# Weight chunks of four 128x512 blocks, one raw tile per seven-product unit, and a residual kept in DRAM during the FFNs

## The chip, the cores and the metric

The kernel runs on one core of a Trainium2 chip. The metric is the device time of one execution in microseconds (us), as the median of several runs. TensorE is written PE, its loads of the stationary operand PEld, VectorE DVE, ScalarE ACT, GpSimd POOL and SyncE SP. SP issues nearly all DMAs.

## The reference, cut to what matters

One layer: a half-step gated FFN, a mixer of two gated linear attentions, a second half-step FFN, each with a norm before and after and a residual. 256 rows, width 2048, FFN width 5504, float32.

```python
def swiglu(x, w_gate, w_up, w_down):
    return (jax.nn.silu(x @ w_gate) * (x @ w_up)) @ w_down

f1 = swiglu(rms_norm(h, ffn1_pre_norm), ffn1_w_gate, ffn1_w_up, ffn1_w_down)
h = h + 0.5 * rms_norm(f1, ffn1_post_norm)
m = hybrid_token_mixer(rms_norm(h, mix_pre_norm), ...)   # proj = u @ w_in; two scans; two branches; w_out
h = h + rms_norm(m, mix_post_norm)
f2 = swiglu(rms_norm(h, ffn2_pre_norm), ffn2_w_gate, ffn2_w_up, ffn2_w_down)
h = h + 0.5 * rms_norm(f2, ffn2_post_norm)
```

## The kernel before, in words

**Split products.** A float32 product is made of three matmuls of a rounded format: each operand is split into `hi`, its rounded value, and `lo = x - hi`; the sum is hi*hi + lo*hi + hi*lo (`mm3`, L155 to L159). Weights come from DRAM into `raw` tiles. ACT writes `whi` as a rounding copy (L151) and DVE subtracts to get `wlo` (L153). All weights are read once, so all of them go through this splitting.

**Tiles.** Rows are two tiles of 128 (`t`), the contraction goes in k-tiles of 128 (`kt`), columns in blocks of 512 (`CB`). A `raw`, a `whi` and a `wlo` tile hold two blocks of 128x512 each (`RW = 2 * CB`), and there are five of each (`RING = 5`). A chunk is two blocks. SP issues a chunk's load as soon as a raw tile is free, so SP runs ahead by the number of raw tiles; ACT and DVE split a chunk as soon as its raw data have landed and a hi/lo pair is free, so they run ahead of PE by the number of hi/lo pairs.

**Two column blocks at a time.** `gemm_pair` makes two column blocks together (gate and up, or two blocks of `w_in`). The contraction is in units `u` of two k-tiles. A plain unit is 2 matrices x 2 k-tiles x 2 row tiles x 3 matmuls, that is 24 matmuls, done in two halves of one matrix each. A unit in `sevens` is a 2x2x2 block product by seven products in place of eight (`Blocks.seven`, L265): 21 matmuls, but three sums of weight blocks (`wsum`) are added on DVE and split as well. `SUMS` has three such units of eight, `FOUR` four. In an FFN they alternate from one pair to the next, the first pair has none; in the mixer, eight of the ten pairs use `SUMS` and two `FOUR`. `gemm_pair` writes the order of the plain halves and of the sevens out by hand (`steps`, `at`); with `late` the sevens come at the end. After the last unit, `share` and `close` add the shared products to the results on DVE. `following` splits the first chunks of the next pair before the closing sums.

**FFN.** Eleven pairs make the gated activations in `hT` (11 tiles, through silu on ACT, one product on DVE into `hn`, and transposes on PE). `down_proj` takes 43 k-tiles by two halves of 1024 columns, `hf`, with six seven-product units in each. The last seven k-tiles of the second half (`DTAIL`) are split ahead and kept, in ring tiles and in tiles that hold nothing else by then (`homes`), because their matmuls come in four passes, one for each row tile and column block.

**Mixer.** `gemm_block` with `held` makes a block for row tile 0 while row tile 1's input is still being settled. Ten pairs of `w_in` blocks follow with the attention between them as side work (`side.pump`), then four `w_branch_gla` and four `w_branch_hgrn` blocks, and `out_proj`. The residual `h` (8 tiles of 128x512) stays on chip in the FFNs; at the mixer's start it is stored to `away` in DRAM, and `h` serves as scratch.

**Order.** Instructions are issued in each engine's queue in an order that a list scheduler fixes at compile time, by the order in which the program states them and by when their inputs would be ready. At run time each queue is in order. DMAs on SP wait in its queue for their raw tile.

Of the kernel before, what the change touches and what calls it, by code (L numbers as in the profile page):

```python
# [7 lines left out]
F32 = mybir.dt.float32  # L8
# [7 lines left out]
P = 128  # L16
# [11 lines left out]
RW = 2 * CB  # L28
STEPS = ((3, 2, 2, 2), (6, 1, 1, 1))
RING = 5  # L30
AHEAD = 3
# [55 lines left out]
def kernel(ctx: ExitStack, tc: tile.TileContext, a: dict, out: bass.AP):  # L87
# [22 lines left out]
    h = [[hpool.tile([P, CB], F32, name=f"h{t}_{n}") for n in range(4)] for t in range(NT)]  # L110

    away = [[dram.tile([P, CB], F32, name=f"away{t}_{n}") for n in range(4)] for t in range(NT)]
# [10 lines left out]

    def ring_alloc(w):
        hi, lo = [ring.tile([P, RW], F32R, tag=s, name=nm(s))[:, :2 * w]
                  .rearrange("p (i c) -> p i c", i=2) for s in ("whi", "wlo")]
        return [(hi, lo)]

    def wload(src: bass.AP, w: int, apart=False):
        raw = ring.tile([P, RW], F32, tag="raw", name=nm("raw"))[:, :2 * w].rearrange(  # L130
            "p (i c) -> p i c", i=2)
        for i in range(2) if apart else [slice(0, 2)]:
            nc.sync.dma_start(raw[:, i, :], src[:, i, :])
        return raw, apart

    def wchunk(src: bass.AP, w: int, alloc=ring_alloc, raw=None):


        raw, apart = raw or wload(src, w)
        parts = alloc(w)  # L140
        if len(parts) == 1:
            hi, lo = parts[0]
            for i in range(2) if apart else [slice(0, 2)]:
                split_into(hi[:, i, :], lo[:, i, :], raw[:, i, :])
            return [(hi[:, i, :], lo[:, i, :]) for i in range(2)]
        for i, (hi, lo) in enumerate(parts):
            split_into(hi, lo, raw[:, i, :])
        return parts
# [12 lines left out]
    def gemm_block(w_dram, c0, w, lhs, nkt=KT, held=None, raws=(), ready=()):  # L161
# [4 lines left out]
        raws, ready = list(raws), list(ready)  # L166
        nb = -(-w // CB)
        step = 2 // nb
        pss = [[ps_tile(f"mm{t}") for _ in range(nb)] for t in range(NT)]

        def chunk(k0, alloc):
            if ready:
                return ready.pop(0)
            raw = raws.pop(0) if raws else None
            src = w_dram[k0 * P:(k0 + step) * P, c0:c0 + w]
            return wchunk(src.rearrange("(k p) c -> p k c", p=P) if nb == 1 else
                          src.rearrange("p (n c) -> p n c", n=nb), w // nb, alloc, raw)

        def mm(t, k0, parts):
            for i, part in enumerate(parts):  # L180
                kt = k0 + i % step
                mm3(pss[t][i // step][:, :w // nb], lhs(t, kt), part, kt == 0, kt == nkt - 1)

        if held is None:
            for k0 in range(0, nkt, step):
                parts = chunk(k0, ring_alloc)
                for t in range(NT):
                    mm(t, k0, parts)
                side.pump()
        else:  # L190
            kept = []
            for i, k0 in enumerate(range(0, nkt, 2)):
                kept.append((k0, chunk(k0, ring_alloc if i < RING else held)))
                mm(0, *kept[-1])
                side.pump()
            for k in kept:
                mm(1, *k)
                side.pump()
# [46 lines left out]
    class Blocks:  # L245
# [19 lines left out]
        def seven(self, u, end):  # L265
            w, k0 = self.w, 2 * u
            ra, rb = [ring.tile([P, RW], F32, tag="raw", name=nm("raw"))[:, :2 * w]
                      .rearrange("p (i c) -> p i c", i=2) for _ in range(2)]
            wsum, hi, lo = [row_tile(n, d)[:, :, :w] for n, d in
                            (("wsum", F32), ("wsumh", F32R), ("wsuml", F32R))]  # L270

            nc.sync.dma_start(ra[:, 0, :], self.block(0, k0))
            nc.sync.dma_start(ra[:, 1, :], self.block(1, k0 + 1))
            nc.sync.dma_start(rb[:, 0, :], self.block(1, k0))
            nc.sync.dma_start(rb[:, 1, :], self.block(0, k0 + 1))
# [8 lines left out]
            last[0] = nc.scalar.activation(hi[:, 2, :], wsum[:, 2, :], AF.Copy)  # L284
# [4 lines left out]
            first, second, third = [[(part[0][:, i, :], part[1][:, i, :]) for i in range(n)]  # L289
                                    for part, n in (((ahi, alo), 2), ((bhi, blo), 2), ((hi, lo), 3))]  # L290
# [5 lines left out]
            self.product((0, 0), self.lhs(0, k0 + 1), second[1])  # L296
            side.pump()
            self.product("p6", self.part("s2", u), second[0], end)
            self.product("p5", self.part("d", u), third[0], end)
            self.product("p7", self.part("s3", u), third[1], end)  # L300
# [1062 lines left out]
```

## Time and profile before

| | |
|---|---|
| median of 3 runs | 2080.19 us (2079.95 to 2080.34) |
| profiled execution | 2080.67 us |
| span of its instructions | 2078.8 us |
| PE busy | 2067.8 us (99%), 10509 matmuls |
| DVE busy | 1854.7 us (89%), 2187 instructions |
| ACT busy | 1239.7 us (60%), 1670 instructions |
| DMA | 412.23 MB, 198 GB/s in the mean |

A row of groups gives line, engine, operation, the tiles as out<-in, the shape and the number of instructions; then busy time and mean ns of one; then the idle time of the engine just before them and what ended most of it. A row of waits gives who waited <- for whom: us in total, times, longest. A row of the timeline gives start and duration. A row of stretches gives busy time (and count) of each engine, the granted clock of PE, the DMA share and GB/s. Durations of matmuls overlap; their price is the distance of their starts.

### The profile page before, as it was taken

To read this page: it belongs to the slowest core of one execution; us is meant where nothing else is said; L and a number is where in the kernel's file an instruction comes from. 1 tells how busy PE (TensorE), PEld (TensorE's weight loads), DVE (VectorE), ACT (ScalarE), POOL (GpSimd) and SP (SyncE) were. 2 spreads that over 40 slices of the span, in tenths; PEclk is the share of its full clock that TensorE was granted. 3 is DMA by queue.
4 is the path that set the end of the run, shared out by engine and by line. 5 is a ranking of instruction groups with operands and counts; after the bars stand their busy time and mean duration, and the time that the engine had idled before them with its cause. 6 is when DMAs were issued, how large, how long until landed. Compare 5 with 4: busy or idle time off the path is not lost.

```text
span 2078.8 us, 29319 instructions
## 1 busy us (share of the span) xinstructions
PE 2067.8 (99%) x10509; PEld 1721.1 (83%) x10509; DVE 1854.7 (89%) x2187; ACT 1239.7 (60%) x1670; POOL 40.6 (2%) x87
## 2 busy tenths in 40 slices
PE   9999999999999999999999999999999999999998
PEld 7888888898888888878888888888888888898886
DVE  7898999989999879989999897578999989999896
ACT  6555656565666576576655554465555655666663
POOL 1000000000000100000000000010000000000000
PEclk9999999999999999999999999999999999999999
DMA  8566656656667467555565666755666657576663
GB/s 267 183 210 199 211 188 194 214 183 226 208 195 233 153 192 232 163 168 188 174 203 186 184 221 214 220 179 172 222 200 186 209 186 224 165 239 201 198 208 132
DMA packets 200665, 412.23 MB, mean 198 GB/s; under 512 B 18036, under 2 KB 26423, under 8 KB 200520
## 3 DMA queue, kind: packets, MB, share of 16 engines
q1 hardware_dynamic: 194896, 401.80, 61.0%
q10 hardware_dynamic: 5624, 8.57, 1.3%
q8 instruction: 82, 1.34, 0.3%
q14 instruction: 63, 0.52, 0.1%
HBM read 406.11 MB, written 4.19 MB: 197 GB/s over the span
## 4 chain that ended last, share of the span: by engine, by line
PE 96%; ACT 1%; DVE 1%; issue 0%; DMA 0%; POOL 0%; SPq 0%; DVEq 0%; POOLq 0%; ACTq 0%
PE c L157 22%; PE c L159 21%; PE c L158 21%; PE p L159 5%; PE p L158 5%; PE p L157 5%; PE mm L157 3%; PE mm L159 3%; PE mm L158 3%; PE ps L397 2%; PE acc L157 1%; PE acc L158 1%; PE acc L159 1%; PE ps L905 0%; DVE h L510 0%
## 5 line engine op out<-in xcount | busy, mean ns | idle before, releaser
L151 ACT ACTIVATE whi<-raw 128x1024 fp32r<-128x1024 f32 (+3 forms) x498 | 510.6, 1033 | 279.8 <-PE c L158 114.7
L153 DVE TENSOR_TENSOR wlo<-raw,whi 128x1024 fp32r<-128x1024 f32 (+3 forms) x498 | 587.5, 1190 | 86.6 <-ACT whi L151 85.3
L157 PE MATMUL c<-whi,xhi 128*128 128x512 f32 (+1 forms) x1270 | 495.8, 391 | 0.5 <-DVE hq L849 0.3
L159 PE MATMUL c<-wlo,xhi 128*128 128x512 f32 (+1 forms) x1270 | 490.8, 387 | 0.0
L158 PE MATMUL c<-whi,xlo 128*128 128x512 f32 (+1 forms) x1270 | 490.5, 386 | 0.0
L243 DVE TENSOR_TENSOR wlo<-raw,whi 128x1024 fp32r<-128x1024 f32 (+1 forms) x252 | 294.5, 1203 | 11.9 <-ACT whi L278 6.3
L159 PEld LDWEIGHTS c<-wlo,xhi 128*128 128x128 f32 x1270 | 238.4, 188 | 47.2 <-DVE wlo L153 0.3
L157 PEld LDWEIGHTS c<-whi,xhi 128*128 128x128 f32 x1270 | 238.5, 188 | 46.9 <-issue 0.7
L158 PEld LDWEIGHTS c<-whi,xlo 128*128 128x128 f32 x1270 | 238.6, 188 | 44.9
L282 ACT ACTIVATE whi<-raw 128x1024 fp32r<-128x1024 f32 (+1 forms) x126 | 131.8, 1046 | 204.5 <-DVE raw L243 78.5
L243 DVE TENSOR_TENSOR wsuml<-wsum,wsumh 128x1536 fp32r<-128x1536 f32 (+1 forms) x126 | 218.0, 1730 | 33.7 <-ACT wsumh L284 33.6
L157 PE MATMUL c<-whi,hkhi 128*128 128x512 f32 x558 | 217.0, 389 | 0.0
L159 PE MATMUL c<-wlo,hkhi 128*128 128x512 f32 x558 | 216.8, 388 | 0.0
L158 PE MATMUL c<-whi,hklo 128*128 128x512 f32 x558 | 216.7, 388 | 0.0
L280 ACT ACTIVATE wsumh<-wsum 128x1024 fp32r<-128x1024 f32 (+1 forms) x126 | 131.5, 1044 | 108.6 <-DVE wsum L243 74.7
L278 ACT ACTIVATE whi<-raw 128x1024 fp32r<-128x1024 f32 (+1 forms) x126 | 131.4, 1043 | 100.2 <-PE c L158 84.7
L243 DVE TENSOR_TENSOR wsum<-raw,raw 128x1024 f32<-128x1024 f32 (+1 forms) x126 | 151.8, 1205 | 20.5 <-DMA raw<-in_ffn_w_down_dram 17.3
L159 PEld LDWEIGHTS c<-wlo,hkhi 128*128 128x128 f32 x558 | 104.8, 188 | 21.6
L158 PEld LDWEIGHTS c<-whi,hklo 128*128 128x128 f32 x558 | 104.8, 188 | 21.3
L157 PEld LDWEIGHTS c<-whi,hkhi 128*128 128x128 f32 x558 | 104.8, 188 | 21.3
L243 DVE TENSOR_TENSOR c<-c,psum 128x512 f32<-128x512 f32 (+1 forms) x135 | 86.6, 682 | 11.8 <-PE c L159 11.4
L243 DVE TENSOR_TENSOR wsum<-raw 128x512 f32<-128x512 f32 (+1 forms) x126 | 86.0, 683 | 3.6
(347 smaller groups left out, 3117.1 us busy)
## 6 DMA issues: line engine op xcount, KB each, us to landing
raw<-in_ffn_w_down_dram SPq DMA_DIRECT2D x124, 512.0 KB, 4.6
raw<-in_w_in_dram SPq DMA_DIRECT2D x104, 512.0 KB, 4.5
raw<-in_ffn_w_up_dram SPq DMA_DIRECT2D x97, 512.0 KB, 4.5
raw<-in_ffn_w_gate_dram SPq DMA_DIRECT2D x96, 512.0 KB, 4.7
raw<-in_ffn_w_gate_dram SPq DMA_DIRECT2D x128, 256.0 KB, 3.8
raw<-in_w_in_dram SPq DMA_DIRECT2D x128, 256.0 KB, 3.5
raw<-in_ffn_w_up_dram SPq DMA_DIRECT2D x126, 256.0 KB, 3.8
raw<-in_ffn_w_down_dram SPq DMA_DIRECT2D x96, 256.0 KB, 4.0
```

Of the source, the lines that this page charges most:

```text
L151: last[0] = nc.scalar.activation(hi, src, AF.Copy)
L153: nc.vector.tensor_tensor(lo, src, hi.bitcast(F32), op=ALU.subtract)
L157: nc.tensor.matmul(ps, lhsT=xhi, rhs=whi, start=start, stop=False)
L158: nc.tensor.matmul(ps, lhsT=xlo, rhs=whi, start=False, stop=False)
L159: nc.tensor.matmul(ps, lhsT=xhi, rhs=wlo, start=False, stop=stop)
L243: return nc.vector.tensor_tensor(o, x, y, op=op)
L278: nc.scalar.activation(ahi, ra, AF.Copy)
L280: nc.scalar.activation(hi[:, 0:2, :], wsum[:, 0:2, :], AF.Copy)
L282: nc.scalar.activation(bhi, rb, AF.Copy)
L397: end = nc.tensor.transpose(dst_ps[:, i * P:(i + 1) * P], src[:, i * P:(i + 1) * P], ident)
```

## The change

`RW` becomes `4 * CB`: raw, hi and lo tiles hold four blocks. There are three hi/lo pairs (`RING = 3`) and two raw tiles (`RAWS = 2`). The residual becomes two tiles `hrow` of 128x2048, of which `h[t][n]` are slices, under the tag `hold`; while `roomy` is set, in an FFN from its second pair on, these two serve as raw tiles three and four in turn. The second FFN stores the residual to `away2` first; `residual()` loads it back (in the first FFN from `x`) after unit 6 of the second half of `down_proj`, and from there on `roomy` is off. A plain unit is one chunk of both matrices, loaded by two DMAs and split by one ACT and one DVE instruction; in `seven`, all four blocks are in one raw tile, rearranged so that three are split to `hi` by one instruction, and `lo` by one. `gemm_block`, `out_proj` and `down_proj` take chunks of four blocks as well. The FFN's `hn` is gone, its product overwrites silu's tile; `hT` has 10 tiles, its last part lies in `xlo0`; the mixer has 31 tiles `b` for 33.

```diff
-RW = 2 * CB
+RW = 4 * CB
-RING = 5
-AHEAD = 3
+RING = 3
+RAWS = 2
+AHEAD = 2
...
+    def new_h():
+        for t in range(NT):
+            hrow[t] = hpool.tile([P, 4, CB], F32, tag="hold", name=nm(f"h{t}"), bufs=NT)
+            h[t] = [hrow[t][:, n, :] for n in range(4)]
...
+    def raw_tile(w):
+        turn[0] += 1
+        if roomy[0] and turn[0] % (RAWS + NT) >= RAWS:
+            raw = hpool.tile([P, RW], F32, tag="hold", name=nm("raw"), bufs=NT)
+        else:
+            raw = ring.tile([P, RW], F32, tag="raw", name=nm("raw"), bufs=RAWS)
+        return raw[:, :4 * w].rearrange("p (i c) -> p i c", i=4)
...
+    def split(raw, w, n=4, alloc=ring_alloc):
+        parts, at = [], 0
+        for hi, lo in alloc(w):
+            m = min(hi.shape[1], n - at)
+            split_into(hi[:, :m, :], lo[:, :m, :], raw[:, at:at + m, :])
+            parts += [(hi[:, i, :], lo[:, i, :]) for i in range(m)]
+            at += m
         return parts
...
         def seven(self, u, end):
-            ra, rb = [ring.tile([P, RW], F32, tag="raw", name=nm("raw"))[:, :2 * w]
-                      .rearrange("p (i c) -> p i c", i=2) for _ in range(2)]
...
-            (ahi, alo), (bhi, blo) = ring_alloc(w) + ring_alloc(w)
-            nc.scalar.activation(ahi, ra, AF.Copy)
-            add(wsum[:, 0:2, :], ra, rb[:, 0:1, :].broadcast_to([P, 2, w]))
-            nc.scalar.activation(hi[:, 0:2, :], wsum[:, 0:2, :], AF.Copy)
-            add(rb[:, 0, :], wsum[:, 0, :], ra[:, 1, :])
-            nc.scalar.activation(bhi, rb, AF.Copy)
-            summed = add(wsum[:, 2, :], rb[:, 0, :], rb[:, 1, :])
-            last[0] = nc.scalar.activation(hi[:, 2, :], wsum[:, 2, :], AF.Copy)
+            raw = raw_tile(w)
...
+            for j, (i, k) in enumerate(((0, k0), (1, k0 + 1), (0, k0 + 1), (1, k0))):
+                load(raw, j, self.block(i, k))
+
+            hi, lo = ring_alloc(w)[0]
+            nc.scalar.activation(hi[:, 0:3, :], raw[:, 0:3, :], AF.Copy)
+            add(wsum[:, 0:2, :], raw[:, 0:2, :], raw[:, 3:4, :].broadcast_to([P, 2, w]))
+            add(raw[:, 3, :], wsum[:, 0, :], raw[:, 1, :])
+            nc.scalar.activation(hi[:, 3, :], raw[:, 3, :], AF.Copy)
+            summed = add(wsum[:, 2, :], raw[:, 3, :], raw[:, 2, :])
+            last[0] = nc.scalar.activation(shi, wsum, AF.Copy)
             with tc.issue_after(summed.ins):
-                add(alo, ra, ahi.bitcast(F32), ALU.subtract)
-            add(blo, rb, bhi.bitcast(F32), ALU.subtract)
-            add(lo, wsum, hi.bitcast(F32), ALU.subtract)
+                add(lo, raw, hi.bitcast(F32), ALU.subtract)
+            add(slo, wsum, shi.bitcast(F32), ALU.subtract)
...
+    def load_unit(ws, u, w):
+        raw = raw_tile(w)
+        for i, (w_dram, c0) in enumerate(ws):
+            load(raw, slice(2 * i, 2 * i + 2), rows_of(w_dram, 2 * u, 2, c0, w))
+        return raw
+
+    def unit_of(*ws, w=CB):
+        return lambda: split(load_unit(ws, 0, w), w)
...
             k0 = 2 * u
-            parts = ready.pop(0) if ready else split(i, k0)
-            if (u, i) == (nu - 1, 0) and sevens:
-                ready = [split(1, k0)]
-                b.share()
+            if i == 0:
...
+                    parts = ready or split(load_unit(ws, u, w), w)
+                    ready = None
+                if u == nu - 1 and sevens:
+                    b.share()
...
             for t in range(NT):
-                b.plain((k0, k0 + 1), t, i, parts, u == nu - 1)
+                b.plain((k0, k0 + 1), t, i, parts[2 * i:2 * i + 2], u == nu - 1)
...
-        def split(hf, kt, alloc=ring_alloc):
-            return wchunk(w_dram[kt * P:(kt + 1) * P, hf * 1024:(hf + 1) * 1024]
-                          .rearrange("p (n c) -> p n c", n=2), CB, alloc)
+        def chunk(hf, kt, n=2, alloc=ring_alloc):
+            raw = raw_tile(CB)
+            nc.sync.dma_start(raw[:, :2 * n, :].rearrange("p (k n) c -> p k (n c)", n=2),
+                              rows_of(w_dram, kt, n, hf * 1024, 1024))
+            return split(raw, CB, 2 * n, alloc)
...
+                if hf and u == 6:
+                    residual()
...
+                    for t in range(NT):
+                        nc.sync.dma_start(away2[t], hrow[t])
...
+            def residual():
+                roomy[0] = False
+                new_h()
+                for t in range(NT):
+                    nc.sync.dma_start(hrow[t], a["x"][t * P:(t + 1) * P, :].rearrange(
+                        "p (n c) -> p n c", c=CB) if begin else away2[t])
 
             return down_proj(a[pre + "_w_down"], FKT, lhs, sums_of, post, pre_next,
                              [wpost[:, n, :] for n in range(4)], ys,
-                             [held_x] + [ring_alloc] * 2 + [held] * 4, then)
+                             [(1, held_x), (2, ring_alloc), (4, held)], residual, then)
...
-                return b2.tile([P, CB], dt, tag="b", name=nm(s), bufs=33)
+                return b2.tile([P, CB], dt, tag="b", name=nm(s), bufs=31)
```

More of the change, by code (lines that the diff above doesn't have):

```diff
@@ L624, in down_proj @@
             units = sorted(DSUMS + DMORE[hf])
-            kt = 0
-            while kt < n:
-                u = kt // 2
-                if kt % 2 == 0 and u + 1 in units and u + 1 not in parts:
+            for kt in range(0, n, 2):
+                u, m = kt // 2, min(2, n - kt)
+                if u + 1 in units and u + 1 not in parts:
                     parts[u + 1] = sums_of(u + 1)
@@ L652, in down_proj @@
         tail = []
[L653 to L656 removed]
+        kt = nkt - DTAIL
+        for m, home in homes:
+            for j in range(0, m, 2):
+                got = chunk(1, kt, min(2, m - j), home)
+                for k in range(0, len(got), 2):
+                    tail.append((kt, got[k:k + 2]))
+                    lhs_h(0, kt)
+                    kt += 1
         for t in range(NT):
```

277 lines of the change are left out of this document (141 added, 136 removed).

## Prediction

> **What bounds the kernel now.** I read the page's busy lines first, then the chain that ended last.
>
> ```profile
> span 2078.8 us, 29319 instructions
> PE 2067.8 (99%) x10509; PEld 1721.1 (83%) x10509; DVE 1854.7 (89%) x2187; ACT 1239.7 (60%) x1670; POOL 40.6 (2%) x87
> PE 96%; ACT 1%; DVE 1%; issue 0%; DMA 0%; POOL 0%; SPq 0%; DVEq 0%; POOLq 0%; ACTq 0%
> ```
>
> PE is busy 99% and is 96% of the chain. A busy PE could still be a stretched one, so the timeline of PE comes next: first and last row of an unbroken run of 29 matmuls.
>
> ```profile
> 199.65 0.39 PE L159 MATMUL c<-wlo,xhi 128*128 128x512 f32 x1
> ...
> 205.99 0.39 PE L157 MATMUL c<-whi,hkhi 128*128 128x512 f32 x1
> ```
>
> 28 steps in 6.34 us are 0.2264 us from start to start: the 0.39 is a pipelined duration, 0.2264 is the price. Next, the waits of PE (all it has) and stretches of equal length.
>
> ```profile
> PE ps L1303 <- POOL idle L1298: 1.3, 1, 1.3
> PE ps L965 <- ACT state L975: 0.4, 1, 0.4
> PE c L157 <- DVE hq L849: 0.3, 1, 0.3
> PE ps L1307 <- DMA ident<-in_c_ident_dram: 0.2, 1, 0.2
> ```
>
> ```profile
> 200.00:250.00 50.00, 50.00 (x227) 41.49 (x226) 49.16 (x49) 30.36 (x35) 0.00 (x0) 1.00 0.65 205
> 950.00:1000.00 50.00, 50.00 (x469) 40.68 (x468) 49.47 (x81) 32.93 (x52) 0.99 (x2) 1.00 0.54 169
> 1100.00:1150.00 50.00, 50.00 (x342) 40.74 (x340) 47.80 (x61) 25.82 (x31) 0.00 (x0) 1.00 0.59 190
> 2050.00:2078.80 28.80, 20.27 (x90) 16.46 (x88) 12.85 (x20) 3.20 (x9) 2.12 (x7) 0.92 0.20 73
> ```
>
> Columns: PE, PEld, DVE, ACT, POOL, clock, DMA share, GB/s. PE waits 2.2 us in all; outside the first microseconds and the last 8.5 (28.80 - 20.27) it has nothing to give back. DVE is the second bound, over 94% busy in the gated-pair stages, yet never late. So an edit that leaves the matmuls as they are can gain only at the two ends, and can lose wherever an operand comes late.
>
> **The change, part by part.** The matmuls and their number stay: 24 per plain unit (5.43 us at 0.2264) and 21 per seven-product unit (4.75 us). What changes is the grain of splitting, the number of tiles, and the residual.
>
> *Merged splits.* Groups of instructions, shapes kept apart:
>
> ```profile
> L153 DVE TENSOR_TENSOR wlo<-raw,whi 128x1024 fp32r<-128x1024 f32 x462 | 558.2, 1218 | 76.3 <-ACT whi L151 75.1
> L151 ACT ACTIVATE whi<-raw 128x1024 fp32r<-128x1024 f32 x462 | 484.5, 1056 | 261.9 <-PE c L158 108.2 <-issue 35.3 <-PE mm L158 33.7
> L243 DVE TENSOR_TENSOR wsuml<-wsum,wsumh 128x1536 fp32r<-128x1536 f32 x119 | 208.6, 1753 | 33.3 <-ACT wsumh L284 33.1
> L243 DVE TENSOR_TENSOR wsum<-raw,raw 128x1024 f32<-128x1024 f32 x119 | 145.2, 1220 | 20.5 <-DMA raw<-in_ffn_w_down_dram 17.3 <-DMA raw<-in_w_in_dram 1.6 <-DMA raw<-in_ffn_w_up_dram 0.2
> L243 DVE TENSOR_TENSOR wsum<-raw 128x512 f32<-128x512 f32 x119 | 82.1, 690 | 3.4
> L284 ACT ACTIVATE wsumh<-wsum 128x512 fp32r<-128x512 f32 x119 | 73.5, 618 | 8.3 <-DVE wsum L243 8.3
> ```
>
> Another 512 columns cost DVE 0.53 us (1753 - 1220) and ACT 0.44 (1056 - 618), so estimates for 128x2048 are 2.29 us on DVE and 1.93 on ACT, for 128x1536 on ACT 1.49. A plain unit: DVE 2.29 for 2 x 1.218, ACT 1.93 for 2 x 1.056. A seven: DVE 1.22 + 2 x 0.69 + 2.29 + 1.75 = 6.64 for 6.79, ACT 1.49 + 0.62 + 1.49 = 3.60 for 3.79. DVE saves 0.15 x 231 + 0.15 x 126 = 54 us, which I cost at nothing for the span: PE's unbroken 0.2264 covers it all. [...] What it costs is grain: the first piece of a chunk is usable after 1.93 + 2.29 = 4.22 us instead of 2.27.
>
> *Three hi/lo tiles in the four-seven blocks.* In the order written for FOUR, units come as 0, 1 (first half), seven 2, 1 (second half), seven 4, 3 (first half), seven 5, 3, seven 6, 7. Before, the halves were chunks of their own in five pairs of tiles; now a unit's tile is held over the seven between its halves, and with three tiles unit 3 takes the tile of unit 1. It is free when PE has done unit 1's second half; only seven 4 (4.75 us) lies before unit 3, whose lo is first read two matmuls later: 5.20 us, of which 4.22 are needed. 0.98 is left for two semaphores and whatever DVE is in the middle of: at 49.16 of 50 us busy, often seven 5's lo (2.29) or sums' lo (1.75). So a stall between 0 and 1.3 us (2.29 - 0.98), once per such block; there are five in each FFN and two in the mixer. I take the middle, 0.6: 12 x 0.6 = 7 us, ends 0 and 16.
>
> *Two raw tiles in the mixer* (2 x 4 blocks, where there were 5 x 2). SP's queue and the landings:
>
> ```profile
> 202.43 0.38 SPq L133 DMA_DIRECT2D raw<-in_ffn_w_gate_dram  x1
> 203.53 0.38 SPq L133 DMA_DIRECT2D raw<-in_ffn_w_up_dram  x1
> 217.08 0.33 SPq L274 DMA_DIRECT2D raw<-in_ffn_w_up_dram  x1
> 217.46 1.35 SPq L275 DMA_DIRECT2D raw<-in_ffn_w_gate_dram  x1
> ```
>
> ```profile
> raw<-in_w_in_dram SPq DMA_DIRECT2D x104, 512.0 KB, 4.5
> raw<-in_w_in_dram SPq DMA_DIRECT2D x128, 256.0 KB, 3.5
> SPq L133 <- DVE wlo L153: 539.0, 288, 17.2
> ```
>
> SP now waits 539 us for raw tiles, 17.2 at most: loads are issued as tiles come free, and landed data lies waiting. A plain unit's two 512 KB loads are issued 1.1 us apart and land 1.1 + 4.5 = 5.6 us after the first; a seven's four of 256 KB, 0.38 apart, after 3 x 0.38 + 3.5 = 4.6. A plain tile is then taken for 5.6 + 1.93 + 2.29 = 9.8 us, a seven's for 4.6 + 1.22 + 2 x 0.69 + 2.29 = 9.5. Two tiles give a unit per 4.9 us at best; PE takes one per (5 x 5.43 + 3 x 4.75)/8 = 5.17. The spare 0.27 per unit, 0.54 per tile, is what a split may wait behind other work on DVE. At 47.8 and 49.5 of 50 busy it waits behind half an operation as a rule (0.6 of 1.2 us), which eats the spare; two such waits per tile overdraw it by 0.33 per unit. The mixer's ten pairs are 80 units: 0 to 80 x 0.33 = 26 us; nearer the lower end, since PE's attention work lengthens its time per unit too: 8 us. [...]
>
> *End of each down projection.* From unit 6 of the second half on, the residual has its tiles again, so only two raw tiles are left, and the seven last k-tiles must all be split before the first of four tail passes.
>
> ```profile
> 2020.56 23.04 SPq L133 DMA_DIRECT2D raw<-in_ffn_w_down_dram  x11
> 2048.90 2.35 DVE L153 TENSOR_TENSOR held<-raw,held 128x1024 fp32r<-128x1024 f32 x2
> 2051.72 0.42 DVE L153 TENSOR_TENSOR hklo<-hT,hkhi 128x256 fp32r<-128x256 f32 x1 [0.47 <-ACT hkhi L151]
> 2051.07 0.39 PE L157 MATMUL c<-held,hkhi 128*128 128x512 f32 x1
> ```
>
> PE enters the tail at 2051.07 and takes a k-tile per 3 x 0.2264 = 0.68; the last is wanted at 2055.1 and was ready at 2052.1. After the change: unit 17 can be split when unit 14's tile is free, at the start of seven 15 (2051.07 - 2 x 5.43 - 4.75 = 2035.5), so by 2039.7. Its raw tile then takes k-tiles 37 and 38: 2039.7 + 9.8 = 2049.5; the same tile then takes 41 and 42: with 5.6 + 1.06 + 1.22 for the first, 2057.4, wanted at 2051.07 + 5 x 0.68 + 0.45 = 2054.9. That is 2.5 us late, twice in the kernel: 5 us; ends 0 (DVE further ahead) and 12 (one more queued operation of each unit before it).
>
> *Residual.* Two 1 MB stores at the start of ffn2 and two 1 MB loads in each FFN, on SP's queue. In the queue the loads wait for the last two borrowed raw tiles (units 3 and 4), and unit 7's load waits behind them. The stores lie beside the second pass over held weights (16 k-tiles, 10.9 us, wants no load): nothing. The loads:
>
> ```profile
> DMA packets 200665, 412.23 MB, mean 198 GB/s; under 512 B 18036, under 2 KB 26423, under 8 KB 200520
> q1 hardware_dynamic: 194896, 401.80, 61.0%
> ```
>
> 198 GB/s at about 0.62 of the engines is 320 at full, so 2.1 MB take 6.6 us and unit 7's blocks land 12.2 after unit 4's split, usable after 12.2 + 1.22 + 2 x 0.69 + 2.29 = 17.1; PE has units 4, 5 and 6 in hand, 5.43 + 4.75 + 5.43 = 15.6. Up to 1.5 late, nothing if DVE leads: 0.5 each, 1 us. With the cover gone it is the whole 6.6.
>
> *Costed at nothing:* the product of up, silu and rstd now written over silu's tile (the same four tiles, and DVE still waits for the same operands); the regrouped start of the first FFN, since the blocks that the first matmuls want are issued in the old order; 31 instead of 33 mixer tiles, since the held weights take four fewer (8 for 12). Each could hide +-1 us.
>
> **Sum.** 7 + 8 + 5 + 1 = 21 us of new PE waiting, minus nothing. The profiled execution took 2080.67 us (span 2078.8), 0.5 above the median of 2080.19: 2080.2 + 21 = 2101 us.
>
> **The rivals.**
> 1. *Nothing is late: not slower.* From this profile: DVE gets 54 us of air, four raw tiles of four blocks in the FFNs are 16 blocks where there were 10, and the instruction order can put the urgent split first. It decides if unit 3's split always finds DVE free within 0.98 us and mixer tiles wait under 0.54. Against it: DVE at 49.16 of 50, hardly a moment free. Time: 2081.
> 2. *The mixer becomes bound by its loads.* If each split waits twice on DVE, 26 in place of 8, and w_out's and the branches' 32 units (plain, 5.43 against 4.9) lose 0.3 each as well: 21 + 18 + 10, 2129. For it: 9.8 us taken of at most 10.3. Against: before, 17.2 us of SP waiting show data lying idle for long.
> 3. *Faster.* PE can give back only its 2.2 us of waits and part of the last 8.5, whose chain the change leaves alone: with all of the first and half of the last, 2080 - 2.2 - 4.3 = 2074. Nothing speaks for it but DVE being freer at the last closing sums.
> 4. *The clock falls in a stall.* The last stretch shows 0.92 granted with PE idle for 8.5 us, a loss of 0.08 x 28.8 = 2.3 us; the others 1.00. If the four stalls at the ends of the down projections and at the residual grow by 1.5 us each and each loses as much clock: 2101 + 4 x 3.8 = 2116. [...]
>
> **How the numbers follow.** Forecast (2085 to 2118 its own range, central 2101): 0.48. Rival 1: 0.20. Rival 2: 0.20. Rival 3: 0.05. Rival 4: 0.07. Faster by over 0.2% (4.2 us, about what a measurement of this kernel can tell): 0.05, rival 3; within: 0.20; slower: 0.48 + 0.20 + 0.07 = 0.75. Range 2080 to 2129: it leaves out rival 3, some of rival 1 and the worse half of rival 2, 0.2 in all.
>
> **What would show it.** Right: PE waits in the low twenties of us, many of 0.3 to 1.3 on a unit's lo just after a seven in every second FFN block; in the mixer, more waits of ACT and DVE for raw tiles' DMAs than before; a wait of 2 to 3 us where each down projection enters its tail; DVE's busy time down by some 54 us; SP waiting much less for raw tiles. Wrong: PE's waits as short as now (rival 1), mixer stretches with PE and DVE both idle on loads (rival 2), or a start-to-start time of matmuls other than 0.2264, on which every term rests.

## The result, and the profile after

The changed kernel takes 2134.5 us (median of 4 runs, 2133.3 to 2136.7), the kernel before 2080.3 beside it (2080.0 to 2081.7): a ratio of 1.026, 95% interval 1.024 to 1.028. The prediction had 2101, at most 2129: the direction was right, the size was not. The profiled execution took 2133.3 us. (One execution of a later kernel, e1_late, took 11969 us with 512-column matmuls 1.28 us apart; it is left out of the comparison, and that kernel was run again for its trace.) First its busy lines and the chain that ended last:

```profile
span 2131.6 us, 27517 instructions
PE 2089.2 (98%) x10509; PEld 1723.2 (81%) x10509; DVE 1835.4 (86%) x1812; ACT 1198.4 (56%) x1295; POOL 48.5 (2%) x87
PE 71%; DVE 11%; DMA 9%; ACT 5%; issue 3%; SPq 1%; POOL 0%; DVEq 0%; ACTq 0%; POOLq 0%
```

The same 10509 matmuls, 52.8 us more of span. PE is only 71% of the chain where it was 96%, and DMA is 9% of it where it was 0. PE was also busy 21.4 us longer (2089.2 for 2067.8), and idle 31.4 longer (42.4 for 11.0). Stretches tell where: first four of the changed kernel, then four of the kernel before with the same work in them (columns as in the prediction).

```profile
50.00:590.00 540.00, 540.00 (x2470) 453.14 (x2469) 494.05 (x432) 309.74 (x285) 1.31 (x2) 1.00 0.62 203
590.00:692.00 102.00, 96.47 (x415) 78.22 (x414) 77.46 (x72) 52.02 (x50) 0.00 (x0) 0.98 0.55 182
692.00:724.00 32.00, 26.80 (x117) 20.69 (x116) 27.77 (x35) 20.55 (x37) 9.50 (x17) 0.89 0.51 174
724.00:1316.00 592.00, 577.25 (x3672) 465.59 (x3671) 513.75 (x603) 344.85 (x446) 17.79 (x24) 0.99 0.56 180
```

```profile
49.00:589.00 540.00, 540.00 (x2469) 453.17 (x2468) 498.15 (x536) 320.29 (x387) 0.50 (x2) 1.00 0.63 201
589.00:682.50 93.50, 93.50 (x413) 77.28 (x412) 85.83 (x95) 59.38 (x73) 0.38 (x2) 1.00 0.71 227
682.50:707.00 24.50, 24.36 (x120) 19.49 (x119) 22.11 (x34) 15.55 (x36) 8.12 (x17) 1.00 0.37 124
707.00:1272.40 565.40, 564.65 (x3668) 466.60 (x3668) 515.52 (x703) 353.86 (x547) 14.44 (x22) 1.00 0.61 189
```

Five hundred and forty us of the first FFN cost not a tenth of a us more: there four raw tiles exist. The second half of its down projection (590 to 692), the step to the mixer (692 to 724) and the mixer lose 8, 8 and 27 us: there two exist. In the two long ones of these rows PE, DVE and the DMAs all have a smaller busy share than before; in the step to the mixer PE and DVE do, while the DMAs carry more (0.51 for 0.37). That suggests a wait that goes round: nobody is the bound, each waits for the other. The stall below shows one.

To lay the runs side by side I took the start of the k-th 512-column matmul in each trace minus that in the kernel before, for those k that end a stage there. The gain of that lag in each stage, in us:

| kernel | start | FFN 1, to mid-down | its 2nd half | step to mixer | mixer | out_proj | FFN 2, to mid-down | its 2nd half |
|---|---|---|---|---|---|---|---|---|
| changed | 1.2 | 0.0 | 8.2 | 7.7 | 26.7 | 0.0 | 0.0 | 8.3 |
| e2_noborrow | 1.2 | 29.4 | 10.9 | 8.4 | 31.0 | 0.1 | 28.8 | 7.7 |
| e1b_late | 1.0 | 0.0 | -0.1 | -0.9 | 29.1 | -0.1 | 0.0 | 0.0 |
| e7_splitonly | 0.0 | 0.0 | 6.5 | -1.2 | 27.4 | -0.2 | 0.0 | 5.3 |
| e6b_halves | -0.1 | 0.0 | 5.3 | -1.7 | 2.4 | -0.2 | 0.0 | 0.0 |
| e10_halves_late | 0.1 | 0.0 | -0.1 | -1.7 | 4.2 | -0.2 | 0.0 | 0.0 |
| e4_before4 | 0.0 | 1.2 | 6.3 | 0.0 | 3.0 | 0.0 | 0.0 | 0.0 |
| e5_before3 | 0.0 | 54.8 | 21.5 | -0.8 | 44.6 | 9.7 | 55.3 | 13.0 |

Then one stall from end to end, in the second half of the first down projection of the changed kernel. SP's queue, ACT, DVE and PE in that order:

```profile
628.37 1.77 SPq L150 DMA_DIRECT2D raw<-in_ffn_w_down_dram  x4
632.57 0.38 SPq L629 DMA_DIRECT2D raw<-in_ffn_w_down_dram  x1
638.87 1.75 SPq L150 DMA_DIRECT2D raw<-in_ffn_w_down_dram  x4
642.74 0.38 SPq L629 DMA_DIRECT2D raw<-in_ffn_w_down_dram  x1
...
633.30 1.49 ACT L291 ACTIVATE whi<-raw 128x1536 fp32r<-128x1536 f32 x1 [3.08 <-DMA raw<-in_ffn_w_down_dram]
645.19 1.48 ACT L291 ACTIVATE whi<-raw 128x1536 fp32r<-128x1536 f32 x1 [5.29 <-DMA raw<-in_ffn_w_down_dram]
646.58 0.61 ACT L164 ACTIVATE hkhi<-sums 128x512 fp32r<-128x512 f32 x1
...
633.90 1.23 DVE L259 TENSOR_TENSOR wsum<-raw 128x1024 f32<-128x1024 f32 x1 [1.35 <-DMA raw<-in_ffn_w_down_dram]
636.55 2.29 DVE L259 TENSOR_TENSOR wlo<-raw,whi 128x2048 fp32r<-128x2048 f32 x1
640.43 2.28 DVE L166 TENSOR_TENSOR wlo<-raw,whi 128x2048 fp32r<-128x2048 f32 x1
```

```profile
644.63 0.39 PE L172 MATMUL c<-wsuml,hkhi 128*128 128x512 f32 x1
647.77 0.49 PE L170 MATMUL c<-whi,hkhi 128*128 128x512 f32 x1 [2.75 <-ACT hkhi L164]
648.58 0.79 PE L171 MATMUL c<-whi,hklo 128*128 128x512 f32 x1 [0.31 <-DVE hklo L166]
649.60 0.63 PE L170 MATMUL c<-whi,hkhi 128*128 128x512 f32 x1
650.02 0.63 PE L171 MATMUL c<-whi,hklo 128*128 128x512 f32 x1
```

The first raw tile is asked for at 628.37. Its data let ACT begin at 633.30, DVE's last read of it (the wlo that starts at 636.55) ends at 638.84, and at 638.87 SP issues the next load into it: 10.5 us. The other tile goes from 632.57 to the end of the wlo at 642.71, 10.1. Two tiles thus give two units in some 10.3 us, and PE needs 5.43 + 4.75 = 10.18 for a plain one and a seven. Nothing is spare, and each delay stays. The next seven's data are such a delay: asked for at 638.87, they let ACT begin 6.3 us later, where the seven before took 4.9. At 645.19 ACT has waited 5.29 us for them; behind it in ACT's queue stand the `hkhi` copies of the unit before, whose inputs were there, and it is these that PE waits for, 2.75 us. After the stall matmuls start 0.425 us apart for a while (649.60, 650.02), not 0.2265: the granted clock is 0.50 from 648.14 to 651.56, a second loss. There are six such pieces of 3.41 us in this execution before its end, two of them together (at 648.14, 706.17, 764.20, 863.18 and 2068.09). PE is busy for 18.3 us in them, so half of that, some 9 us of the 52.8, is the clock's; this is an estimate. The four largest groups of PE's waits (who <- for whom: us, times, longest) show the same two kinds: copies of activations behind a split that waits for its load, and wlo itself.

```profile
PE c L170 <- ACT hkhi L164: 6.4, 2, 3.6
PE p L172 <- DVE wlo L259: 6.1, 5, 1.6
PE mm L170 <- ACT xhi L164: 3.5, 1, 3.5
PE c L172 <- DVE wlo L166: 3.4, 4, 1.6
```

### The profile page after: what moved, and what is told of

It reads as the page before. It is cut to its first block, busy times and chain, and to the rows that moved or that the text cites. A ratio compares the mean times of both kernels' runs of the same rounds, so it can differ in the third digit from the quotient of the medians.

```text
span 2131.6 us, 27517 instructions
## 1 busy us (share of the span) xinstructions
PE 2089.2 (98%) x10509; PEld 1723.2 (81%) x10509; DVE 1835.4 (86%) x1812; ACT 1198.4 (56%) x1295; POOL 48.5 (2%) x87
## 4 chain that ended last, share of the span: by engine, by line
PE 71%; DVE 11%; DMA 9%; ACT 5%; issue 3%; SPq 1%; POOL 0%; DVEq 0%; ACTq 0%; POOLq 0%
PE c L172 16%; PE c L170 16%; PE c L171 16%; DMA raw<-in_w_in_dram 6%; PE p L172 4%; PE p L170 4%; PE p L171 4%; DVE wlo L259 3%; DMA raw<-in_ffn_w_down_dram 2%; DVE wlo L166 2%; ACT whi L164 2%; DVE wsum L259 2%; PE ps L421 2%; PE mm L170 2%; PE mm L171 2%
## 5 line engine op out<-in xcount | busy, mean ns | idle before, releaser
L164 ACT ACTIVATE whi<-raw 128x2048 fp32r<-128x2048 f32 (+4 forms) x254 | 469.7, 1850 | 405.6 <-PE c L171 102.3
L166 DVE TENSOR_TENSOR wlo<-raw,whi 128x2048 fp32r<-128x2048 f32 (+4 forms) x254 | 558.9, 2202 | 124.2 <-ACT whi L164 121.2
L259 DVE TENSOR_TENSOR wlo<-raw,whi 128x2048 fp32r<-128x2048 f32 (+1 forms) x126 | 284.8, 2261 | 55.3 <-ACT whi L294 54.9
L291 ACT ACTIVATE whi<-raw 128x1536 fp32r<-128x1536 f32 (+1 forms) x126 | 185.4, 1471 | 205.9 <-PE c L171 63.4
L259 DVE TENSOR_TENSOR wsum<-raw 128x1024 f32<-128x1024 f32 (+1 forms) x252 | 238.1, 945 | 24.4 <-DMA raw<-in_w_in_dram 10.8
L296 ACT ACTIVATE wsumh<-wsum 128x1536 fp32r<-128x1536 f32 (+1 forms) x126 | 185.0, 1468 | 27.4 <-DVE wsum L259 24.1
L294 ACT ACTIVATE whi<-raw 128x512 fp32r<-128x512 f32 (+1 forms) x126 | 78.0, 619 | 99.2 <-DVE raw L259 99.0
L259 DVE TENSOR_TENSOR psum<-psum,p 128x512 f32<-128x512 f32 (+2 forms) x102 | 86.5, 848 | 3.1 <-PE p L172 1.8
```

What stands on the lines that cost most here:

```text
L164: last[0] = nc.scalar.activation(hi, src, AF.Copy)
L166: nc.vector.tensor_tensor(lo, src, hi.bitcast(F32), op=ALU.subtract)
L259: return nc.vector.tensor_tensor(o, x, y, op=op)
L291: nc.scalar.activation(hi[:, 0:3, :], raw[:, 0:3, :], AF.Copy)
L294: nc.scalar.activation(hi[:, 3, :], raw[:, 3, :], AF.Copy)
L296: last[0] = nc.scalar.activation(shi, wsum, AF.Copy)
```

## The experiments

Theory A: two raw tiles, taken whole for load and split, make the loads late wherever only two exist; A1 says that their bytes are too few, A2 that the grain of release is too coarse. B: the long merged splits do it in the queues of ACT and DVE. C: the residual's loads do it. D: the clock adds to each stall.

**e1_late**

```diff
-                if hf and u == 6:
-                    residual()
...
+        residual()
         for t in range(NT):
             for n in (2, 3):
```

> The changed kernel with one call moved: the residual is loaded back only when the seven last k-tiles of the second half of a down projection have been split, so that the two borrowed raw tiles stay in use to there. Theory A (two raw tiles, each taken whole for load and split, some 10.3 us, are too slow wherever only two exist): the second halves of both down projections lose nothing more, that is 8.2 + 8.1 us back, 2134.5 - 16 = 2118; the transition to the mixer (7.7) and the mixer (26.7) stay as they are. Theory B (the merged splits and their order in the queues of ACT and DVE do the damage, however many raw tiles there are): the stalls of 1.5 to 3 us on whi and hkhi stay, 2134 +- 3. Theory C (the 2 MB of residual, loaded in between the weights, makes them late): the loads move into the tail, where nothing waits for weights, so 2118 as well; e2_noborrow tells it from A.

2109.0 us, ratio 1.014 (1.013 to 1.016): 25.5 back where A had 16. The trace by stage is that of e1b_late, the same kernel.

**e1b_late**

> e1_late once more, for its trace by stage. It took 2109.0, 25.5 us less than the changed kernel, where theory A had 16 from the two second halves. If the transition from the first down projection to the mixer (7.7 us lost in the changed kernel) hangs on the same two raw tiles, it shows nothing lost here either: 16.5 + 7.7 = 24.2, and the rest of the loss, some 27, lies in the mixer alone.

2109.6, a single execution. As A had it: the second halves and the step to the mixer lose nothing (-0.1, -0.9 and 0.0 in the table), and 29 of its 29.0 us are the mixer's. Long splits alone are thus not the cause there: they are as long as they were.

**e2_noborrow**

```diff
-                roomy[0] = True
...
-                        nc.sync.dma_start(away2[t], hrow[t])
...
-                new_h()
-                for t in range(NT):
-                    nc.sync.dma_start(hrow[t], a["x"][...] if begin else away2[t])
```

> The changed kernel without borrowing: the residual stays on chip in the FFNs, is neither stored nor loaded again, and there are two raw tiles everywhere. Theory A: the gated pairs and the first halves of the down projections, which lost nothing with four raw tiles, lose as the mixer does, 26.7 us in 592, that is 4.5% of about 1140 us, 51 us: 2134.5 + 51 = 2185. Theory B: they lose nothing, as their splits are the same: 2134 or less. Theory C: the second halves of the down projections get their 16 us back: 2118.

2197.1, ratio 1.057 (1.055 to 1.059): 62.6 slower, where A had 51 and C 16 faster. C has fallen: without any load of the residual the second halves lose 10.9 and 7.7 all the same. The FFNs, which lost nothing with four raw tiles, now lose 29 us each.

**e4_before4**

```diff
-    raw = ring.tile([P, RW], F32, tag="raw", name=nm("raw"))
+    raw = ring.tile([P, RW], F32, tag="raw", name=nm("raw"), bufs=4)
```

(the same for the sevens' `ra` and `rb`)

> The kernel before with four raw tiles of two blocks in place of five: the same 2 MB of raw room as the changed kernel has in the mixer, in the old grain. Theory A1 (too few bytes in flight): the mixer loses as it does in the changed kernel, and so do the FFNs: 2080 + 27 at least, up to 2080 + 90. Theory A2 (the grain: a tile is held whole until its four blocks are split): a tile of two blocks is taken for 4.5 + 1.06 + 1.22 = 6.8 us, four of them give one per 1.7 us, and PE takes one per 2.6: 2080 to 2085. Theory B says 2080 too.

2092.3, ratio 1.006 (1.004 to 1.007). The bytes of the changed kernel in the old grain cost 12 us, not 54, and the mixer 3.0, not 26.7. A2 is nearer, but 2080 to 2085 was too low: 6.3 of it lie in the second half of the first down projection.

**e6_halves and e6b_halves**

```diff
-            raw = ring.tile([P, RW], F32, tag="raw", name=nm("raw"), bufs=RAWS)
-        return raw[:, :4 * w].rearrange("p (i c) -> p i c", i=4)
+        return [ring.tile([P, 2 * CB], F32, tag="raw", name=nm("raw"), bufs=2 * RAWS)[:, :2 * w]
+                .rearrange("p (i c) -> p i c", i=2) for _ in range(n // 2)]
```

(and a DMA and a split for each half)

> The changed kernel with its two raw tiles of the ring cut into four of two blocks, each loaded, split and released by itself (hi and lo tiles still of four blocks, the borrowed tiles still whole). Theory A2: a half is taken for 6.8 us in place of 10.3, the loads are no longer late in the mixer nor in the second halves of the down projections: 2134.5 - 27 - 16 - 5 = about 2086. Theory A1 (bytes): as the changed kernel, 2134 +- 5. Theory B (merged splits and the order): the splits from the ring are two-block ones again, so much of the loss goes here too, but with the three hi/lo tiles of four blocks left, PE should still wait on wlo behind sevens.

> The same edit as e6_halves, with the first pair's second half written to its own column block again (in e6_halves it went to the first one's; the instructions are the same in number and shape). The same time is expected by every theory: 2085.5 +- 1.5.

2085.5, and 2086.2 in the second form, ratio 1.003 (1.002 to 1.004). The first form leaves the first pair's second column block out; the second, which is the kernel compared from here on, writes it. The two are the same in time, as expected. 48 of the 54 us are back, in the mixer 24 of 27. Of the waits on wlo that B expected from the three hi/lo tiles one of 0.3 us comes.

**e7_splitonly**

```diff
-        return [ring.tile([P, 2 * CB], F32, tag="raw", ..., bufs=2 * RAWS)[:, :2 * w]
-                .rearrange("p (i c) -> p i c", i=2) for _ in range(n // 2)]
+        raw = ring.tile([P, RW], F32, tag="raw", name=nm("raw"), bufs=RAWS)
+        return [raw[:, 2 * i * w:2 * (i + 1) * w].rearrange("p (i c) -> p i c", i=2)
+                for i in range(n // 2)]
```

(against e6b_halves)

> The same instructions as e6b_halves (loads and splits of two blocks from the ring), but the raw tile is one of four blocks again, two of them: it is released only when both its halves are split. The two kernels differ in nothing but when raw room comes free. Theory A2 (the raw tile held whole): the tile is taken for 5.6 + 1.06 + 2 x 1.22 = 9.1 us in place of 9.8 (10.3 measured), so something of the loss comes back, but most stays: 2134.5 - 20 = 2115, anything from 2100 to 2130. Theory B (the long merged splits in the queues of ACT and DVE, not the release): as e6b_halves, 2085 +- 4.

2122.3, ratio 1.020 (1.018 to 1.021): 36 us above its twin, which issues the same loads and splits. (The scheduler places some of DVE's and ACT's instructions elsewhere in their queues; what that is worth was not tried by itself.) The mixer of each, e7_splitonly first:

```profile
713.00:1304.00 591.00, 572.12 (x3668) 464.85 (x3666) 517.90 (x702) 349.09 (x515) 17.00 (x22) 1.00 0.57 180
...
711.00:1280.00 569.00, 567.00 (x3681) 468.41 (x3680) 518.22 (x705) 350.32 (x516) 15.29 (x22) 1.00 0.60 189
```

DVE does the same 518 us of work in both; PE is idle 19 us in one, 2 in the other. B has fallen for the mixer: finer splits of a tile that is held whole recover nothing there (27.4 for 26.7). It is the release. Elsewhere the long splits have a part: with finer ones the step to the mixer loses nothing (-1.2 for 7.7) although the tiles are still held whole, and the second halves lose 6.5 and 5.3 for 8.2 and 8.3. The step's loss thus goes away with more raw tiles (e1b_late) and also with finer splits.

**e10_halves_late**

> e6b_halves and e1_late together: raw room in halves, and the borrowed tiles kept until the tail's splits. e6_halves lost 4.9 us in the second half of the first down projection and 1.1 in that of the second, both at the tail's start. Theory A: with four blocks' worth more of raw room there, these go: 2085.5 - 6 = 2079.5, level with the kernel before. If the rest of the loss is from the three hi/lo tiles or from the residual's loads falling into the next stage, it stays at 2083 to 2086.

2081.5, ratio 1.0004 (0.9995 to 1.0013): no difference from the kernel before. The end of the down projections is clean (-0.1, 0.0), and 4.2 in the mixer is what remains.

**e5_before3**: as e4_before4, with `bufs=3`.

> The kernel before with three raw tiles of two blocks, 1.5 MB in all, a quarter less than the changed kernel's two of four. Theory A1 (the bytes of raw room decide): it must lose more than the changed kernel did, so 2132 or more. Theory A2 (the grain decides): a tile is taken for some 6.8 us, three give one per 2.27, and PE takes one per 2.6 (5.17 per unit of two): 0.3 to spare where five tiles had 1.2, so it loses more than with four tiles (2092) and less than the changed kernel: 2095 to 2120.

2279.6, ratio 1.097 (1.095 to 1.098), worse than every other kernel. My sum for A2 has failed, and A1's sign was right. The rows of SP, ACT and DVE show what the sum left out, one seven and the plain tile before it:

```profile
1001.04 0.38 SPq L133 DMA_DIRECT2D raw<-in_w_in_dram  x1
1004.76 0.33 SPq L272 DMA_DIRECT2D raw<-in_w_in_dram  x1
...
1005.89 0.33 SPq L274 DMA_DIRECT2D raw<-in_w_in_dram  x1
...
1008.70 15.92 SPq L133 DMA_DIRECT2D raw<-in_w_in_dram  x7
...
1004.70 1.05 ACT L151 ACTIVATE whi<-raw 128x1024 fp32r<-128x1024 f32 x1
1005.78 1.75 DVE L243 TENSOR_TENSOR wsuml<-wsum,wsumh 128x1536 fp32r<-128x1536 f32 x1
1007.45 1.22 DVE L153 TENSOR_TENSOR wlo<-raw,whi 128x1024 fp32r<-128x1024 f32 x1
...
1012.34 2.35 DVE L243 TENSOR_TENSOR wlo<-raw,whi 128x1024 fp32r<-128x1024 f32 x2
```

A seven takes two tiles. The first is held from 1004.76 to the end of its wlo at 1013.56, the second from 1005.89 to 1014.69: 8.8 us each, not 6.8. A plain tile goes from 1001.04 to 1008.67, 7.6, because its wlo stands behind the wsuml of the seven before on DVE. So neither bytes nor grain alone decide; what fits these kernels is **room against rate times hold**. PE takes 4 blocks in 5.17 us, 0.77 per us. Rate times hold is the room that is needed. In the mixer of each of these kernels SP asks for the next load as soon as a tile is free, so all the room is always taken and what is in use tells nothing. A block is held 5/8 x 7.6 + 3/8 x 8.8 = 8.1 us in the fine grain, so room for 6.2 blocks is needed: with 6 the mixer loses 44.6 us, with 8 it loses 2.4 to 4.2 (e4_before4, e6b_halves, e10_halves_late), with 10, the kernel before, PE waits for no weight there. In the coarse grain the hold is 5/8 x 10.1 + 3/8 x 10.5 = 10.25, so 7.9 blocks are needed of the 8 that there are: 26.7. These are estimates from holds of single tiles, the coarse ones from the down projection. They put these kernels in the order measured; the size of a loss they do not give.

**e12_gaps and e13_gaps2** (the second's edit; both on the kernel before)

```diff
+    def gap(n):
+        for i in range(2):
+            ps = ps_tile("gap")
+            with tc.issue_after(held_up[0].ins) if i else nullcontext():
+                held_up[0] = nc.tensor.transpose(ps[:32, :P], dead, ident)
+            for _ in range(0 if i else n):
+                nc.gpsimd.memset(dead, 0.0)
```

> The kernel before with one gap put into PE's work in each of the ten later pairs of the first FFN: PE transposes a 128x32 tile, GpSimd clears that tile n times (n = 2, 4, 6, 8, 12, 16, 20, 24, 28, 32), PE transposes it again and so must wait. A clear of 512 elements takes 0.53 us and one of a single element 0.10, so one of 32 is some 0.13: gaps of 0.5 to 4.5 us, 23 us in all. Theory D (a stall is followed by matmuls at a lower clock; in the changed kernel PE was busy 21.4 us longer on the same matmuls and idle 31.4 longer, so 0.68 per us of idle time): the first matmuls after the longer gaps start 0.425 us apart, not 0.2265, for some us, and the kernel takes 2080 + 23 x 1.68 = 2119. The rival (a gap costs itself alone): 2103, all starts 0.2265 apart.

2096.0, a single execution, below both. Between 2 and 25 matmuls ran between the two transposes and covered most of each gap; what was left, up to 1.6 us, was followed by no slower start: these stalls cost themselves alone. But one wait of 2.23 us that was not planted (PE for wlo, until 483.88) was followed by granted clock 0.50 from 485.19 to 488.60. So D has fallen for these short gaps only.

> In e12_gaps twelve matmuls were issued between the two transposes, so that the gaps were only 0.3 to 1.6 us, and none of them was followed by slower matmuls; but after 2.4 us at 483.9 two starts were 0.425 apart. Here the two transposes stand next to each other: the first FFN gets single gaps with 3, 5, 7, 8, 9, 10, 12, 16, 22 and 30 clears, that is 0.3 + 0.18 n = 0.8, 1.2, 1.6, 1.7, 1.9, 2.1, 2.5, 3.2, 4.3 and 5.7 us; the second gets two or three gaps in a row, 2.7 us of matmuls apart (five pairs of 2 x 1.2, 1.6, 1.9, 2.3, 2.8; five of 3 x 1.2, 1.6, 1.9, 0.8, 2.3). Theory D with a threshold: single gaps to about 1.7 us cost themselves alone, from about 2 us on each is followed by some 7 starts of 0.425 and costs about 1.4 to 2.2 us beside itself; what several short gaps do is open. The rival (no fall of the clock, only waits for something else): no start of 0.425 after any of them. All gaps together are 25 us in the first FFN and 42 in the second: 2147 if they cost themselves alone, about 2180 with the slower starts.

2169.6, a single execution, between the two. PE's rows about two of the single gaps:

```profile
324.10 0.27 PE L132 MATMUL gap<-ident,dead 128*32 128x128 f32 x1
326.68 0.29 PE L132 MATMUL gap<-ident,dead 128*32 128x128 f32 x1 [2.31 <-POOL dead L134]
...
369.20 0.27 PE L132 MATMUL gap<-ident,dead 128*32 128x128 f32 x1
372.51 0.28 PE L132 MATMUL gap<-ident,dead 128*32 128x128 f32 x1 [3.04 <-POOL dead L134]
373.57 0.62 PE L177 MATMUL c<-whi,xlo 128*128 128x512 f32 x1
373.98 0.63 PE L178 MATMUL c<-wlo,xhi 128*128 128x512 f32 x1
```

After 2.58 us from transpose to transpose, and all shorter single gaps, matmuls start 0.23 apart at once. After 3.31 the first ones do (to 373.57), then eight start 0.41 to 0.43 apart, and the lag grows by 1.7 us beyond the gap, where shorter gaps add 0.1 to 0.2; after 4.41 the same. That looks like a threshold on the length of a gap, but the trace's record of the granted clock shows something else. In it the clock changes only at edges that are whole multiples of 3.413 us apart: half-clock stretches begin at 373.56, 421.35, 1612.60 and 1892.49, and the last three lie 14, 363 and 445 times 3.413 us after the first. Stretches cut at these edges, around the gaps at 324.10, 369.20 and 1889.14 (length, then PE's busy time; the clock is the third figure from the end):

```profile
322.38:325.79 3.41, 1.99 (x14) 1.50 (x12) 3.38 (x4) 3.39 (x6) 0.90 (x8) 1.00 0.42 147
325.79:329.21 3.42, 2.53 (x12) 2.11 (x13) 3.42 (x4) 1.05 (x2) 0.60 (x5) 1.00 0.85 248
329.21:332.62 3.41, 3.41 (x17) 2.83 (x16) 2.67 (x4) 1.38 (x2) 0.00 (x0) 1.00 0.68 207
...
370.15:373.56 3.41, 1.04 (x5) 0.88 (x6) 3.34 (x5) 0.35 (x1) 1.62 (x13) 1.00 0.88 282
373.56:376.98 3.42, 3.42 (x10) 2.67 (x9) 1.65 (x2) 0.15 (x1) 0.00 (x0) 0.50 0.44 115
...
1889.07:1892.48 3.41, 1.28 (x9) 0.95 (x7) 3.41 (x6) 0.90 (x2) 1.38 (x11) 1.00 0.37 121
1892.48:1895.90 3.42, 2.74 (x10) 2.15 (x8) 2.65 (x5) 1.97 (x3) 0.39 (x4) 0.50 0.02 3
```

The gap of 2.58 is cut by an edge: PE is idle for 1.42 us of one stretch and 0.89 of the next, and the clock stays. The gap of 2.40 at 1889.14, with no gap before it, lies in one stretch, with PE idle for 2.13 us, and the next stretch has half the clock. So it is with the two gaps of 2.40 at 1603.80 and 1609.97: the first is cut into 1.70 and 0.43 and does nothing, the second lies whole in a stretch. In this run every stretch with PE idle for 2.02 us or more is followed by one at half clock, and none with 1.76 or less. So D holds, but in this run it goes by PE's idle time between two edges, and a gap of 2.40 us costs itself alone or 1.6 us more.

**e9_beforefour and e11_halves_late_four**

```diff
-                        (FOUR if f0 // CB % 2 == fours else SUMS) if f0 else ())
+                        FOUR if f0 else ())
```

> The kernel before with four seven-product units in each of the twenty later gated pairs, where half of them had three: 10 pairs x 3 matmuls x 0.2265 = 6.8 us less work for PE, 10 x 4.35 us more for DVE. A pair with four has DVE busy 40.9 of 42.6 us in the kernel before, 96%. If five raw tiles of two blocks keep DVE that far ahead pair after pair: 2080.2 - 6.8 = 2073.4. If its lead is used up, PE waits on wlo and wsuml, and it stays at 2078 or more.

> e10_halves_late (2081.5) with the same four units in each pair, the one thing that the merged splits' spared DVE time could buy: 6.8 us less for PE: 2074.7, if DVE, at 46.5 of 50 us with both kinds of pair in turn, keeps ahead at about 48. If not, 2080 or more.

e9_beforefour takes 2074.8, ratio 0.9975 (0.9965 to 0.9984): faster than both kernels. Of the 6.8 us less of matmuls 5.5 arrive, and PE's one new wait stands early in the first down projection (at 467.6), just after the last gated pair:

```profile
PE c L159 <- DVE wlo L153: 1.3, 1, 1.3
```

e11_halves_late_four takes 2084.7, ratio 1.002 (1.001 to 1.003): slower, though DVE is no busier (1887.1 us for 1892.1). In its gated pairs 39 starts are over 0.3 us apart in the stretch from 60 to 440, where the kernel before, e9_beforefour and e10_halves_late have 10. Most of those extra ones are a matmul that comes up to 0.2 us late for a seven's `wlo` and the one after it (149.78, 171.87, 192.18). It differs from e9_beforefour in grain, hi/lo tiles and order together; which of them it is was not tried.

## Why the prediction was wrong, step by step

- **What bounds the kernel**: right. PE starts stayed 0.2265 apart wherever operands were there and the granted clock was 1.00, the change could only lose, and it did.
- **FOUR blocks, 7 us**: measured 0.0. The step that failed is "unit 3 takes the tile of unit 1": I took the tiles by strict turns. In the trace unit 3 is split from 194.26 to 198.50, while PE still reads unit 1 (second half, 196.28 to 199.2) and DVE splits seven 4 (to 196.05). With three tiles it can only lie in that of seven 2, the seven before, whose fourth product reads it last (its wlo at 194.01); the last three products read wsum's. The profile names the load as what ended ACT's wait:

```profile
194.01 0.39 PE L172 MATMUL p<-wlo,hkhi 128*128 128x512 f32 x1
194.26 1.92 ACT L164 ACTIVATE whi<-raw 128x2048 fp32r<-128x2048 f32 x1 [0.53 <-DMA raw<-in_ffn_w_up_dram]
196.21 2.29 DVE L166 TENSOR_TENSOR wlo<-raw,whi 128x2048 fp32r<-128x2048 f32 x1 [0.15 <-PE c L171]
203.75 0.39 PE L170 MATMUL c<-whi,xhi 128*128 128x512 f32 x1
```

  The lo of unit 3 is done at 198.50, 5.7 us before PE reads it (204.21).
- **Mixer, 8 us with ends 0 and 26**: measured 26.7, the upper end. The mechanism was right (tile held against PE's rate); the choice of value failed. The term that was mis-sized is the hold: 9.8 and 9.5 us per tile left 0.54 of spare, and I reckoned the waits on DVE against it. The two tiles of the down projection above took 10.1 and 10.5, a seven's landing 4.9 instead of 4.6 and the rest such waits. In the mixer itself, from 753 to 1100 and where the split had waited for its load, a plain tile was held for 10.3 us (median of 22) and a seven's for 11.2 (of 14), so that 8.2 blocks are needed of 8 by the estimate above: the spare was gone. A single load was in the median no slower than I had it, by the rows of DMA issues of the changed kernel:

```profile
raw<-in_ffn_w_down_dram SPq DMA_DIRECT2D x60, 1024.0 KB, 5.3
raw<-in_w_in_dram SPq DMA_DIRECT2D x96, 512.0 KB, 4.0
```

  From issue to landing 1024 KB took 5.3 us and 512 KB 4.0, for which I had 4.5: the term went to its upper end by the waits.
- **End of the down projections, 5 us, and the residual, 1 us**: measured 8.2 and 8.3. The waits at the tail's start came, 1.1 and 1.5 us of delay where I had 2.5. What I had not costed is that units 7 to 17 go through two raw tiles as the mixer does: the wait of 2.75 at 647.77 is one of these. The stretch was treated by its last tile alone.
- **Costed at nothing**: the step to the mixer, 7.7 us, was no term at all. There ACT waits for w_down's last data with the next stage's `xhi` behind it, and PE for these, 3.5 us; it goes away with more raw tiles (e1b_late) or finer splits (e7_splitonly). The start lost 1.2, just outside my +-1.
- **DVE's 54 us**: busy time fell by 19. In the changed kernel's trace the duration of a split on DVE overlaps its neighbour's by 0.08 us (636.55 + 2.29 ends at 638.84; the next starts at 638.76), so that by my estimate a split less saves about half of what the difference of durations says. For the span it is worth nothing, as forecast.
- **SP waiting much less for raw tiles**, named as a sign of being right, did not come: its waits for wlo are 1471 us in all, where they were 1443. A ring that is refilled as soon as a tile is free made SP wait either way.
- **Rival 2** is what happened in the mixer, though not for w_out, which lost nothing (the branches are within the mixer's 26.7). **Rival 4** happened too: PE's waits of 2.75, 3.49 and 3.64 us (until 647.77, 707.44 and 2067.90) are each followed by slow starts, and so are two in the mixer. That stalls of up to 2.5 us keep the clock, as the central forecast had it, no run shows: in e13_gaps2 a stall of 2.4 kept it or not, as the edges fell.

The sum: 7 + 8 + 5 + 1 = 21 against 0 + 26.7 + 16.5 + 7.7 + 1.2 = 52.1 of the span's 52.8. So three steps came out too small: the hold of a raw tile in the mixer, too short by 0.5 to 1.7 us; two raw tiles through the whole second half of each down projection, reckoned at the tail alone; and the step to the mixer, put at nothing. The FOUR term failed the other way.

## What to carry to other kernels

Count a ring's room against rate times hold, with the hold from the issue of the load to the last read of the whole tile, waits behind other work in the queues included, and do so for each stage by the tiles that it has there: where some 8 of 8 blocks were needed the mixer lost 27 us, where 6.2 of 8 were, it lost 2 to 4. A larger tile that is released whole lengthens the hold at the same bytes, so cut the raw tile finer than the instruction that reads its product if the room is short. And where an engine's queue holds copies for the unit in hand behind a split that waits for a load, the wait for the load can become PE's: ACT's 5.29 us until 645.19 were 2.75 of PE's until 647.77.

## What the runs showed of the hardware

The granted clock changed at edges that are whole multiples of 3.413 us apart (in the changed kernel the half-clock stretches begin 17, 34, 63 and 416 times 3.413 us after the one at 648.14). In e13_gaps2 a stretch between two edges with PE idle for 2.02 us or more was followed by one at half clock, with 1.76 or less it was not; a half-clock stretch full of matmuls was eight starts 0.41 to 0.43 us apart (from 373.57) where 0.2265 is the price, and cost about 1.6 us by that estimate. In the changed kernel two waits of 1.6 and 2.1 us in the mixer (until 763.63 and 863.61) also had such a stretch behind them: PE was idle for 1.72 and 1.87 us between the edges. After 1.27 us idle in a stretch that was itself at half clock (from 706.17) another one followed. A stretch with 1.95 us idle in e5_before3 (701.90) did not bring one. So for 1.7 to 2.0 us of idle time in a stretch at full clock the runs show both; why was not tried.
